# Transposing the softmax weights of 11 heads and three quarters of the feed-forward's tokens with VectorE and HBM in place of TensorE

## The chip, the core and the metric

One core of one Trainium2 chip runs the whole kernel. The metric is device time in microseconds (us). TensorE (PE) multiplies matrices into PSUM and here also transposes 128x128 tiles, VectorE (DVE) and ScalarE (ACT) work elementwise, GpSimd (POOL) helps, and SyncE (SP) issues most of the DMAs. Each engine takes its instructions in order, and the engines wait for each other through semaphores.

## The reference

One layer of an encoder over 256 tokens of width 2048, in float32:

```
h = rmsnorm(x);  q | k | v | u = h @ w_in
scores = q k^T * HEAD_DIM**-0.5 + alibi, masked to |t-s| <= 128
p = exp(scores - m);  p = p / (sum(p) + exp(sink - m))
attention = p v                      (12 query heads, 4 kv heads)
fourier = Re(DFT2(u)) @ w_fourier    (4 groups)
x = x + concat(rmsnorm(attention), rmsnorm(fourier)) @ w_out
g | val = rmsnorm(x) @ w_up;  x = x + (gelu(conv3(g)) * val) @ w_down
y = rmsnorm(x)
```

## The kernel before

Every float32 product is made as three products of rounded halves: an operand is split into `hi` (a copy rounded by ScalarE) and `lo` (the difference, by VectorE). Weights come in units of 1 MB: `load` (line 164) issues the DMA on SP's queue into one of three `raw` buffers, `split` (lines 180 and 181) makes `hi` and `lo`, TensorE multiplies. The order of all work is written out by hand. `unit(i, work)` runs, for unit i: what is listed in `before` (TensorE work of older units), the products of unit i, what is listed in `beside` (VectorE and ScalarE work), `step(i)`, which splits the weights of unit i+2 and then issues the load of unit i+5, and what is listed in `behind`.

Units 0 to 7 are the u and v projections. Units 8 to 23 are the q and k projections, one head each, in the order k, q, q, q for each of four groups. Units 24 to 39 (`N_OUT` is 24) are the output projection, four per chunk of 512 columns. The feed-forward follows.

A query head whose projection is unit s passes through later units: s+1 adds its partial sums (`qk_out`) and splits q (`qk_parts`), s+2 makes the scores on TensorE and, beside them, adds the bias and takes the exponentials (`scores_out`, `exps`), s+3 divides by the sum (`weigh`, line 680), s+4 transposes the 128x512 softmax weights with four TensorE transposes against `ident` (`turn`, line 687) and splits the result out of PSUM into the two tiles `pt` (`turn_out`, lines 699 and 700), s+5 multiplies with v (`values`, line 709) and leaves the result, scaled and split, in a `cat` tile (`values_out`), which the output projection reads. So any unit of the middle stage works on several heads at once.

When a chunk of x is complete (`out_add`, `out_sums`), `turn_x` transposes its 256 tokens by 512 columns with eight TensorE transposes (line 785), and `turn_x_out` scales and splits them into `hT2`, the feed-forward's input (lines 268 and 269). Chunks 0 to 2 do this two units behind the last product; chunk 3 does it in the first step of the feed-forward.

Buffers that matter: `u_hi` and `u_lo` (4 KB per partition each, one buffer) hold the split u until the Fourier group's first product in unit 7; `sc` has four buffers of 2 KB.

Of the kernel before, what the change touches and what calls it, by code (L numbers as in the profile page):

```python
# [8 lines left out]
F32 = mybir.dt.float32  # L9
F32R = mybir.dt.float32r  # L10
AF = mybir.ActivationFunctionType
ALU = mybir.AluOpType

P = 128
D = 2048
S = 256
NK = D // P
HD = 128
NH = 12
# [19 lines left out]
V_G2, V_GA, V_GF, V_DW, V_DB, V_SINK = 0, 16, 28, 32, 161, 204  # L39
# [13 lines left out]
for _g in range(NKV):  # L53
    QK_ORDER += [("k", _g)] + [("q", _g * GQA + _i) for _i in range(GQA)]

QK_FIRST = {n: (2, 2) if n in (8, 12) else (1, 0) for n in range(16)}
N_U, N_V, N_QK = 0, 4, 8
N_OUT = N_QK + len(QK_ORDER)
# [45 lines left out]
def block_kernel(  # L104
# [19 lines left out]
    nc = tc.nc  # L124
    SL = slopes()
    ctx.enter_context(tc.manual_schedule())
    base = ctx.enter_context(tc.tile_pool(name="base", bufs=1))
# [4 lines left out]
    def f32(ap):  # L132
        return ap.bitcast(F32)

    def bank(pool, name):
        return pool.tile([P, 512], F32, tag=pool.name, name=name)
# [29 lines left out]
    def parts_of(i):  # L166
        halves[i] = tuple(
            wp.tile([P, 2176], F32R, tag=h, name=f"{h}{i}", bufs=3)[:, s : s + 2048]
            for h, s in zip(("hi", "lo"), shifts[i])
        )  # L170
        return halves[i]
# [17 lines left out]
    hT = []  # L189
# [10 lines left out]
    xs = [base.tile([P, 2, 512], F32, tag=f"xs{c}", name=f"xs{c}") for c in range(4)]  # L200
# [15 lines left out]
    def u_part(k, o, n, m=1):  # L216

        rows = ux[k // 4][:, (k < 4) * U_HEAD :].rearrange("p (k c) -> p k c", k=4)
        return rows[:, k % 4 : k % 4 + m, o : o + n]
# [43 lines left out]
    def vcol(o, n=1):  # L263
        return vec[:, o : o + n]

    def split_scaled(dst, src, g):

        nc.scalar.activation(dst[:, 0:S], src, AF.Copy, scale=g)
        nc.vector.scalar_tensor_tensor(
            dst[:, S : 2 * S], src, g, f32(dst[:, 0:S]), ALU.mult, ALU.subtract  # L270
        )
# [29 lines left out]
    rows = ctx.enter_context(tc.tile_pool(name="rows", bufs=1, space=bass.MemoryType.DRAM))  # L301

    def row_by_hbm(r, dst, name):
# [2 lines left out]
        nc.gpsimd.dma_start(row.rearrange("b p -> p b"), r)  # L306
        nc.gpsimd.dma_start(dst, row.rearrange("b p -> (b p)").partition_broadcast(P))


    def moving_weights(hi, lo, n, kk, act, b, ps, first, last, q0=0):  # L310

        for q, k in enumerate(kk, q0):
            ah = act(k)[:, b * P : (b + 1) * P]
            al = act(k)[:, S + b * P : S + (b + 1) * P]
            wh, wl = hi[:, q * n : (q + 1) * n], lo[:, q * n : (q + 1) * n]
            nc.tensor.matmul(ps, ah, wh, start=first and q == q0, stop=False)  # L316
            nc.tensor.matmul(ps, al, wh, start=False, stop=False)  # L317
            nc.tensor.matmul(  # L318
                ps, ah, wl, start=False, stop=last and q == q0 + len(kk) - 1
            )  # L320
# [35 lines left out]
    before, beside, behind = {}, {}, {}  # L356

    def at(when, i, f, *a):
        when.setdefault(i, []).append((f, a))
# [13 lines left out]
    for c in range(4):  # L373
        t = base.tile([P, 4, 512], F32R, tag=f"hT{c}", name=f"hT{c}")
        hT.append(t)
    ps_u = [bank(mm, f"ps_u{b}") for b in range(2)]
    for k in range(NK):
        c, q = k // 4, k % 4
        if q == 0:
            hi, lo = (t.rearrange("p (k c) -> p k c", k=4) for t in parts_of(c))  # L380
        n = 1 if c < 2 else 2
# [3 lines left out]
        if q % n == 0:  # L385
            w, h = u_part(k, 0, FW, n), hi[:, q : q + n, :]
# [20 lines left out]
    ph = pa.enter_context(tc.tile_pool(name="pa", bufs=1))  # L407
# [37 lines left out]
    def row_parts(name):  # L445
        return [
            ph.tile([P, 2, FW], F32R, tag=f"{name}_{p}", name=f"{name}_{p}")
            for p in ("hi", "lo")
        ]

    u_hi, u_lo = row_parts("u")
# [157 lines left out]
    qk_sb, st = {}, {}  # L609
    sq_a = ph.tile([P, S], F32, tag="sq", name="sq_a")  # L610

    def qk_out(kind, h, ps):
        tmp = ph.tile([P, S], F32, tag="tmp", name=f"tmp_{kind}{h}", bufs=2)
        nc.scalar.activation(tmp, ps[:, S : 2 * S], AF.Copy)
        add = ph.tile([P, S], F32, tag="add", name=f"add_{kind}{h}", bufs=2)
        nc.vector.tensor_tensor(add, ps[:, 0:S], tmp, ALU.add)
        if kind == "k":
            nc.vector.tensor_tensor(add, add, r1b, ALU.mult)
        st["add", kind, h] = add
# [73 lines left out]
    def turn_out(h):  # L693
# [6 lines left out]
        nc.vector.tensor_tensor(pt[1], ps, f32(pt[0]), ALU.subtract)  # L700
        st["p", h] = pt

    def values(h):
        g = h // GQA
        pt = st.pop(("p", h))
        ps = st["o", h] = bank(dn, f"ps_o{h}")
        for sb in range(2):
            for n, (v, q) in enumerate([(v_hi, 0), (v_hi, 1), (v_lo, 0)]):
                nc.tensor.matmul(  # L709
                    ps[:, 0:S],  # L710
                    v[:, sb, g * HD : (g + 1) * HD],
                    pt[q][:, sb * S : (sb + 1) * S],
                    start=sb == 0 and n == 0,
                    stop=sb == 1 and n == 2,
                )
# [6 lines left out]
    for i in range(N_QK, N_OUT + 8):  # L722
        heads = {i - s: h for (kind, h), s in slot_of.items() if kind == "q"}
        new = [kh for kh, s in slot_of.items() if i - s == 1]
        if 5 in heads:
            at(before, i, values, heads[5])
        if 4 in heads:
            at(before, i, turn, heads[4])
        if 2 in heads:
            at(before, i, scores, heads[2])  # L730
        if 3 in heads:
            at(beside, i, weigh, heads[3])
        for kind, h in new:
            at(beside, i, lambda k=kind, h=h: qk_out(k, h, st.pop(("ps", k, h))))
        if 5 in heads:
            at(beside, i, values_out, heads[5])
        if 4 in heads:
            at(beside, i, turn_out, heads[4])
        for kind, h in new:
            at(beside, i, qk_parts, kind, h)  # L740
        if 2 in heads:
            at(beside, i, scores_out, heads[2])
            at(behind, i, exps, heads[2])

    fourier_channels_steps()
    for n, (kind, h) in enumerate(QK_ORDER):

        def work(hi, lo):
            ps = st["ps", kind, h] = bank(mm, f"ps_{kind}{h}")
            still_weights(hi, lo, ps, range(NK), QK_FIRST[n])  # L750

# [3 lines left out]
    hT2 = []  # L755
# [22 lines left out]
    def turn_x_in(c):  # L778
        pss = []
        for q2 in range(2):  # L780
            ps = bank(dn, f"ps_x{c}{q2}")
            for q in range(2):
                for b in range(2):
                    k4 = 2 * q2 + q
                    nc.tensor.transpose(
                        ps[:, q * S + b * P : q * S + (b + 1) * P],
                        xs[c][:, b, k4 * P : (k4 + 1) * P],
                        ident,
                    )
            pss.append(ps)  # L790
        return pss

    def turn_x_out(c, pss):
        t = base.tile([P, 4, 512], F32R, tag=f"hT{c}", name=f"hU{c}")
        for k4 in range(4):
            ps = pss[k4 // 2][:, k4 % 2 * S : (k4 % 2 + 1) * S]
            split_scaled(t[:, k4, :], ps, vcol(V_G2 + 4 * c + k4))
        hT2.append(t)

    at(before, N_OUT + 6, total, sq_a, "a")  # L800
    at(beside, N_OUT + 6, total_scale, "a", AW)
    ps_a = {}
    for n, (c, kq) in enumerate(OUT_ORDER):
        i = N_OUT + n

        def work(hi, lo):
            if kq == 0:
                ps_a[c] = [bank(mm, f"ps_a{c}{b}") for b in range(2)]
            if kq == 3:
                ps_a[c, "f"] = [bank(dn, f"ps_ff{c}{b}") for b in range(2)]  # L810
            ps = ps_a[c] if kq < 3 else ps_a[c, "f"]
            for b in range(2):
                moving_weights(
                    hi, lo, 512, range(4 * kq, 4 * kq + 4), cat.get, b, ps[b],
                    kq in (0, 3), kq in (2, 3),
                )

        unit(i, work)
        if kq >= 2:
            part = "a" if kq == 2 else "f"  # L820
            ps = ps_a[c] if kq < 3 else ps_a[c, "f"]
            last = c in added
            added.add(c)
            if n == len(OUT_ORDER) - 1:
                later.append(out_post(c, part, ps))
                continue

            at(behind if (c, kq) == (0, 2) else beside, i + 1, out_add, c, part, ps)
            if last:
                at(behind, i + 1, out_sums, c)  # L830
                at(before, i + 2, lambda c=c: st.update({("x", c): turn_x_in(c)}))
                at(beside, i + 2, lambda c=c: turn_x_out(c, st.pop(("x", c))))
    pa.close()
    assert not (before or beside or behind), (before, beside, behind)

# [300 lines left out]
    for q in range(2):  # L1136
        kind, j = items[q]
# [16 lines left out]
    for n, it in enumerate(items):  # L1154
# [8 lines left out]
        if it[0] in ("gate", "val"):  # L1163
            kind, j = it
# [5 lines left out]
        if it[0] == "product":  # L1170
            kind, g, c, p = it
# [13 lines left out]
        else:  # L1185
            kind, c = it
            hi, lo = halves.pop(up_index[n])
# [14 lines left out]
    i = up_index[n]  # L1202
# [35 lines left out]
    x = xs[1][:, 1, :]  # L1238
# [122 lines left out]
```

## Time and profile before

| what | value |
|---|---|
| time, median of 3 runs | 944.87 us (944.45 to 945.13) |
| span of the profiled execution | 943.6 us |
| TensorE busy | 934.2 us, 99% |
| VectorE busy | 759.4 us, 80% |
| ScalarE busy | 542.4 us, 57% |
| GpSimd busy | 50.8 us, 5% |
| granted TensorE clock, mean | 0.998 |
| DMA moved | 214.86 MB |

The profile is one execution. Its span runs from the first to the last instruction; the time of a run includes what lies around that. The page gives busy times by engine and by group of instructions; a group's row names line, engine, operation, output tile<-input tiles, shapes and count, then busy us and mean ns, then the idle time in front of it and what ended it. The chain of waits is the work that ended last, followed back from the last instruction. The timeline lists single instructions with start and length in us; a bracket at its end is the engine's idle time in front of it, with what ended that. DMA rows give the time that SP takes to issue and, apart from it, the time from issue to landing.

### The profile page before, as it was taken

How to read it: one execution, taken by the hardware profiler on the slowest of the kernel's cores; microseconds unless marked ns; L12 is line 12 of the kernel's file. 1: busy time of each engine (PE TensorE's matmuls, PEld its weight loads, DVE VectorE, ACT ScalarE, POOL GpSimd, SP SyncE). 2: the span in 40 equal slices, each digit the busy share in tenths (PEclk: the TensorE clock that was granted, in tenths of full speed). 3: DMA queues.
4: the chain of work that ended last, by engine and by line, in shares of the span. 5: the costliest groups of instructions: out<-in, count | busy, mean ns of one | idle time of the engine just before them, and what ended most of it. 6: DMA issues, size and time to landing. Idle time of an engine off the chain costs nothing.

```text
span 943.6 us, 12812 instructions
## 1 busy us (share of the span) xinstructions
PE 934.2 (99%) x5069; PEld 810.2 (86%) x5069; DVE 759.4 (80%) x946; ACT 542.4 (57%) x662; POOL 50.8 (5%) x68
## 2 busy tenths in 40 slices
PE   9999999999999999999999999999999999999996
PEld 7889998888888888888888888888888888888885
DVE  7658877666677778799887997878989779989886
ACT  7756766554454555566555565555655556655553
POOL 0100000000000000000000000000000000000002
PEclk9999999999999999999999999999999999999999
DMA  9964444445556578877898769877787978779652
GB/s 366 308 223 141 173 140 173 139 174 212 190 215 209 185 232 244 267 257 231 257 266 252 243 236 282 243 262 229 262 242 238 300 245 262 227 234 277 205 179 90
DMA packets 33628, 214.86 MB, mean 228 GB/s; under 512 B 3712, under 2 KB 4224, under 8 KB 10016
## 3 DMA queue, kind: packets, MB, share of 16 engines
q1 hardware_dynamic: 29024, 184.55, 52.8%
q0 software_dynamic: 4544, 29.49, 16.8%
q8 instruction: 40, 0.66, 0.3%
q14 instruction: 20, 0.16, 0.0%
HBM read 211.93 MB, written 2.10 MB: 227 GB/s over the span
## 4 chain that ended last, share of the span: by engine, by line
PE 98%; DVE 1%; DMA 0%; ACT 0%; issue 0%; DVEq 0%; POOLq 0%; POOL 0%; ACTq 0%
PE ps_val L333 25%; PE ps_gate L333 25%; PE ps_q L333 7%; PE ps_P L1070 3%; PE ps_P L1071 3%; PE ps_P L1072 3%; PE ps_N L1070 3%; PE ps_N L1071 3%; PE ps_N L1072 3%; PE ps_a L318 2%; PE ps_k L333 2%; PE ps_a L316 2%; PE ps_a L317 2%; PE ps_s L637 1%; PE ps_o L709 1%; PE ps_ff L316 1%
## 5 line engine op out<-in xcount | busy, mean ns | idle before, releaser
L181 DVE TENSOR_TENSOR lo<-raw,hi 128x2048 fp32r<-128x2048 f32 (+1 forms) x129 | 293.4, 2275 | 44.2 <-ACT hi L180 44.0
L180 ACT ACTIVATE hi<-raw 128x2048 fp32r<-128x2048 f32 (+1 forms) x129 | 245.4, 1903 | 37.8 <-PE ps_a L317 13.5
L333 PE MATMUL ps_val<-hU,hi 128*128 128x512 f32 x688 | 236.2, 389 | 0.0
L333 PE MATMUL ps_gate<-hU,hi 128*128 128x512 f32 x688 | 236.2, 389 | 0.0
L333 PE MATMUL ps_val<-hU,lo 128*128 128x256 f32 x688 | 189.9, 276 | 0.0
L333 PE MATMUL ps_gate<-hU,lo 128*128 128x256 f32 x688 | 189.9, 276 | 0.0
L333 PEld LDWEIGHTS ps_gate<-hU,hi 128*128 128x128 f32 x688 | 129.1, 188 | 26.8
L333 PEld LDWEIGHTS ps_val<-hU,hi 128*128 128x128 f32 x688 | 129.1, 188 | 26.8
L333 PEld LDWEIGHTS ps_gate<-hU,lo 128*128 128x128 f32 x688 | 129.1, 188 | 1.3
L333 PEld LDWEIGHTS ps_val<-hU,lo 128*128 128x128 f32 x688 | 129.1, 188 | 1.3
L845 ACT ACTIVATE ft_g<-ps_gate 128x256 f32<-128x256 f32 x43 | 16.5, 384 | 123.0 <-PE ps_gate L333 123.0
L845 ACT ACTIVATE ft_v<-ps_val 128x256 f32<-128x256 f32 x43 | 16.5, 384 | 91.7 <-PE ps_val L333 91.7
L333 PE MATMUL ps_q<-hT,hi 128*128 128x512 f32 x192 | 65.2, 392 | 0.0
L1070 PE MATMUL ps_P<-hi_P,op_P 128*128 128x512 f32 x144 | 56.0, 389 | 0.0
L1071 PE MATMUL ps_P<-hi_P,op_P 128*128 128x512 f32 x144 | 56.0, 389 | 0.0
L1072 PE MATMUL ps_P<-lo_P,op_P 128*128 128x512 f32 x144 | 56.0, 389 | 0.0
L333 PE MATMUL ps_q<-hT,lo 128*128 128x256 f32 x192 | 51.1, 277 | 0.0
L962 DVE TENSOR_TENSOR lo_N<-sumw,hi_N 128x2048 fp32r<-128x2048 f32 (+1 forms) x20 | 41.5, 2076 | 9.4 <-ACT hi_N L961 9.2
L1070 PE MATMUL ps_N<-hi_N,op_N 128*128 128x512 f32 x108 | 42.0, 389 | 0.0
L1071 PE MATMUL ps_N<-hi_N,op_N 128*128 128x512 f32 x108 | 42.0, 389 | 0.0
L1072 PE MATMUL ps_N<-lo_N,op_N 128*128 128x512 f32 x108 | 42.0, 389 | 0.0
L333 PEld LDWEIGHTS ps_q<-hT,hi 128*128 128x128 f32 x192 | 35.2, 188 | 6.6
(383 smaller groups left out, 1586.9 us busy)
## 6 DMA issues: line engine op xcount, KB each, us to landing
raw<-in_w_up SPq DMA_DIRECT2D x86, 1024.0 KB, 5.8
raw<-in_w_in SPq DMA_DIRECT2D x20, 1024.0 KB, 4.9
raw<-in_w_out SPq DMA_DIRECT2D x16, 1024.0 KB, 4.8
sumw<-in_w_down POOLq DMA_DIRECT2D x16, 1024.0 KB, 8.6
raw<-in_w_down_late SPq DMA_DIRECT2D x4, 1024.0 KB, 6.6
raw<-in_w_down_last SPq DMA_DIRECT2D x4, 768.0 KB, 4.2
ux<-in_w_u_x SPq DMA_DIRECT2D x3, 768.0 KB, 9.2
xs<-in_x SPq DMA_DIRECT2D x4, 512.0 KB, 16.5
```

The lines of the kernel that those rows point to most:

```text
L180: nc.scalar.activation(hi[:, 0:n], raw[:, 0:n], AF.Copy)
L181: nc.vector.tensor_tensor(lo[:, 0:n], raw[:, 0:n], f32(hi[:, 0:n]), ALU.subtract)
L316: nc.tensor.matmul(ps, ah, wh, start=first and q == q0, stop=False)
L317: nc.tensor.matmul(ps, al, wh, start=False, stop=False)
L318: nc.tensor.matmul(ps, ah, wl, start=False, stop=last and q == q0 + len(kk) - 1)
L333: nc.tensor.matmul(ps[:, x], (hi, lo)[i][:, k * P : (k + 1) * P], hk(k)[:, x], start=n == 0 and k == 0, stop=n == len(order) - 1 and k == ...
L637: nc.tensor.matmul(ps[:, b * S : (b + 1) * S], qT[:, qo + b * P : qo + (b + 1) * P], kT[:, ko : ko + S], start=n == 0, stop=n == 2,)
L845: nc.scalar.activation(tmp, ps[:, S : 2 * S], AF.Copy)
L962: nc.vector.tensor_tensor(lo, src, f32(hi), ALU.subtract)
L1070: nc.tensor.matmul(ps, o[:, 0, p, :], hi[:, s], start=first and p == 0, stop=False)
L1071: nc.tensor.matmul(ps, o[:, 1, p, :], hi[:, s], start=False, stop=False)
L1072: nc.tensor.matmul(ps, o[:, 0, p, :], lo[:, s], start=False, stop=last and p == n - 1)
```

## The change

For heads 0 to 10 (`FLIPS`), and for chunks 0 to 2 of x, the TensorE transposes and their PSUM tiles go. In their place VectorE transposes all 32x32 blocks of the tile in one instruction, four DMAs (one per 32 partitions) write these blocks to HBM in runs of 64 floats so that the blocks land in transposed order, and one DMA reads the whole back in runs of 256 floats. The split into `hi` and `lo` then reads SBUF in place of PSUM. Head 11 and chunk 3 stay on TensorE.

For a flipped head, `flip_out` (transpose and writes) stands beside unit s+3, right behind `weigh`; `flip_in` (the read) beside s+4; `flip_parts` (the split) beside s+5; `values` moves from s+5 to s+6. For a chunk, `flip_x_out` stands behind the unit that adds it, `flip_x_in` beside the next and `flip_x_parts` beside the one after. The transposed blocks lie in the buffer of `u_hi` for heads and chunks alike, what comes back in one of `sc` (heads) or in `u_lo` (chunks). All the new DMAs are on SP's queue.

```diff
+FLIPS = range(NH - 1)
...
+    def blocks_out(src, t, name):
+        n = t.shape[1]
+        nc.vector.transpose(t, src)
+        d = rows.tile([n, 32, 4, 64], F32, tag="turn" + name, name="turn" + name, bufs=1)
+        for q in range(4):
+            nc.sync.dma_start(
+                d[:, :, q, :].rearrange("f i r -> i f r"),
+                t[32 * q : 32 * (q + 1)].rearrange("i f b j -> i f (b j)"),
+            )
+        return d
+
+    def blocks_in(d, t):
+        nc.sync.dma_start(t, d.rearrange("(s f) i q r -> (f i) s (q r)", f=4))
...
+    def flip_out(h):
+        sc = st.pop(("sc", h))[0]
+        t = ph.tile([P, 1024], F32, tag="u_hi", name=f"flip{h}")[:, 0:512]
+        t = t.rearrange("p (f b j) -> p f b j", f=8, b=2)
+        st["d", h] = blocks_out(sc.rearrange("p (b f j) -> p f b j", b=2, f=8), t, f"p{h}")
+
+    def flip_in(h):
+        t = ph.tile([P, 512], F32, tag="sc", name=f"flop{h}", bufs=4)
+        t = st["t", h] = t.rearrange("p (s c) -> p s c", s=2)
+        blocks_in(st.pop(("d", h)), t)
+
+    def flip_parts(h):
+        t = st.pop(("t", h)).rearrange("p s (q b j) -> p s b q j", q=4, b=2)
...
+        for s in range(2):
+            nc.scalar.activation(hi[:, s], t[:, s], AF.Copy)
+            nc.vector.tensor_tensor(lo[:, s], t[:, s], f32(hi[:, s]), ALU.subtract)
...
-        if 5 in heads:
-            at(before, i, values, heads[5])
-        if 4 in heads:
+        for n, h in sorted(heads.items()):
+            if n == 5 + (h in FLIPS):
+                at(before, i, values, h)
+        if 4 in heads and heads[4] not in FLIPS:
             at(before, i, turn, heads[4])
...
             at(beside, i, weigh, heads[3])
+            if heads[3] in FLIPS:
+                at(beside, i, flip_out, heads[3])
+        if 4 in heads and heads[4] in FLIPS:
+            at(beside, i, flip_in, heads[4])
...
+        if 5 in heads and heads[5] in FLIPS:
+            at(beside, i, flip_parts, heads[5])
...
+    def flip_x_out(c):
+        t = ph.tile([P, 1024], F32, tag="u_hi", name=f"flipx{c}")
+        t = t.rearrange("p (f b j) -> p f b j", f=16, b=2)
+        src = xs[c].rearrange("p b (f j) -> p f b j", f=16)
+        st["d", "x"] = blocks_out(src, t, f"x{c}")
+
+    def flip_x_in(c):
+        t = ph.tile([P, 1024], F32, tag="u_lo", name=f"flopx{c}")
...
+    def flip_x_parts(c):
...
+        for k in range(4):
...
+            nc.scalar.activation(hi, x[:, k], AF.Copy, scale=g)
+            for b in range(2):
+                nc.vector.scalar_tensor_tensor(
+                    lo[:, b], x[:, k, b], g, f32(hi[:, b]), ALU.mult, ALU.subtract
+                )
...
                 at(behind, i + 1, out_sums, c)
-                at(before, i + 2, lambda c=c: st.update({("x", c): turn_x_in(c)}))
-                at(beside, i + 2, lambda c=c: turn_x_out(c, st.pop(("x", c))))
+                at(behind, i + 1, flip_x_out, c)
+                at(beside, i + 2, flip_x_in, c)
+                at(beside, i + 3, flip_x_parts, c)
```

More of the change, by code (lines that the diff above doesn't have):

```diff
@@ L701, in turn_out @@
         st["p", h] = pt
+    def flip_out(h):
[9 more added lines that the diff above has]
+        t = st.pop(("t", h)).rearrange("p s (q b j) -> p s b q j", q=4, b=2)
+        pt = [
+            ph.tile([P, 512], F32R, tag=f"pt{q}", name=f"pt{q}{h}", bufs=2)
+            for q in range(2)
+        ]
+        hi, lo = (x.rearrange("p (s b q j) -> p s b q j", s=2, b=2, q=4) for x in pt)
+        for s in range(2):
+            nc.scalar.activation(hi[:, s], t[:, s], AF.Copy)
+            nc.vector.tensor_tensor(lo[:, s], t[:, s], f32(hi[:, s]), ALU.subtract)
+        st["p", h] = pt
     def values(h):
@@ L732, in block_kernel @@
             at(beside, i, weigh, heads[3])
+            if heads[3] in FLIPS:
+                at(beside, i, flip_out, heads[3])
+        if 4 in heads and heads[4] in FLIPS:
+            at(beside, i, flip_in, heads[4])
         for kind, h in new:
             at(beside, i, lambda k=kind, h=h: qk_out(k, h, st.pop(("ps", k, h))))
-        if 5 in heads:
-            at(beside, i, values_out, heads[5])
-        if 4 in heads:
+        for n, h in sorted(heads.items()):
+            if n == 5 + (h in FLIPS):
+                at(beside, i, values_out, h)
+        if 4 in heads and heads[4] not in FLIPS:
             at(beside, i, turn_out, heads[4])
+        if 5 in heads and heads[5] in FLIPS:
+            at(beside, i, flip_parts, heads[5])
         for kind, h in new:
@@ L798, in turn_x_out @@
         hT2.append(t)
+    def flip_x_out(c):
[5 more added lines that the diff above has]
+        t = ph.tile([P, 1024], F32, tag="u_lo", name=f"flopx{c}")
+        t = st["x", c] = t.rearrange("p (k c) -> p k c", k=4)
+        blocks_in(st.pop(("d", "x")), t)
+    def flip_x_parts(c):
+        x = st.pop(("x", c)).rearrange("p k (q b j) -> p k b q j", q=4, b=2)
+        t = base.tile([P, 4, 512], F32R, tag=f"hT{c}", name=f"hU{c}")
+        for k in range(4):
+            hi, lo = (
+                t[:, k, p * S : (p + 1) * S].rearrange("p (b q j) -> p b q j", b=2, q=4)
+                for p in range(2)
+            )
+            g = vcol(V_G2 + 4 * c + k)
+            nc.scalar.activation(hi, x[:, k], AF.Copy, scale=g)
+            for b in range(2):
+                nc.vector.scalar_tensor_tensor(
+                    lo[:, b], x[:, k, b], g, f32(hi[:, b]), ALU.mult, ALU.subtract
+                )
+        hT2.append(t)
     at(before, N_OUT + 6, total, sq_a, "a")
```

## The prediction

> **What bounds the kernel now.** I read the page first (span, engines, chain), then the chain of waits by time, then the timelines of VectorE and ScalarE in the projection stage, then the DMA issues.
>
> ```profile
> span 943.6 us, 12812 instructions
> PE 934.2 (99%) x5069; PEld 810.2 (86%) x5069; DVE 759.4 (80%) x946; ACT 542.4 (57%) x662; POOL 50.8 (5%) x68
> PE 98%; DVE 1%; DMA 0%; ACT 0%; issue 0%; DVEq 0%; POOLq 0%; POOL 0%; ACTq 0%
> ```
>
> The chain that ended last is TensorE nearly throughout: what is taken from TensorE is won, if nothing else becomes late. The chain in order of time (start, length, what) gives the price of the transposes:
>
> ```profile
> 78.24 0.72 PE ps_s L637 x6
> ...
> 84.43 0.44 PE ps_t L687 x4
> ...
> 112.35 0.44 PE ps_t L687 x4
> 112.78 0.72 PE ps_s L637 x6
> 113.50 5.45 PE ps_q L333 x32
> 118.95 0.71 PE ps_o L709 x6
> 119.67 0.44 PE ps_t L687 x4
> 120.10 5.48 PE ps_q L333 x32
> ...
> 139.81 0.44 PE ps_t L687 x4
> ...
> 160.38 0.72 PE ps_o L709 x6
> ...
> 187.15 0.71 PE ps_o L709 x6
> ...
> 204.73 0.88 PE ps_x L785 x8
> ```
>
> Each unit is a projection (5.47) with, in front of it, values (`ps_o`, 0.71), transposes (`ps_t`, 0.44 for four) and scores (`ps_s`, 0.72) of older heads. Four units repeat: 112.35 to 139.81 is 27.46 us. VectorE is not idle meanwhile:
>
> ```profile
> core 0: us, PE busy (x) PEld busy (x) DVE busy (x) ACT busy (x) POOL busy (x), PEclk, DMA share, GB/s
> 98.70:126.10 27.40, 27.40 (x178) 24.85 (x176) 22.60 (x51) 18.57 (x36) 2.22 (x3) 1.00 0.44 154
> ```
>
> 22.60 of 27.40 us busy, and much of the rest is waiting inside a ping-pong with ScalarE. That is the second thing to hold against the change. VectorE's timeline, and ScalarE's for the same unit:
>
> ```profile
> 79.81 0.15 DVE L676 TENSOR_TENSOR sm<-sm,ex 128x2 f32<-128x2 f32 x1
> ...
> 86.35 0.16 DVE L676 TENSOR_TENSOR sm<-sm,ex 128x2 f32<-128x2 f32 x1
> ...
> 92.66 0.15 DVE L676 TENSOR_TENSOR sm<-sm,ex 128x2 f32<-128x2 f32 x1
> ...
> 99.64 0.42 DVE L616 TENSOR_TENSOR add_q<-ps_q,tmp_q 128x256 f32<-128x256 f32 x1
> 99.98 0.48 DVE L269 SCALAR_TENSOR_TENSOR cat<-ps_o,vec,cat 128x256 fp32r<-128x256 f32 x1
> ...
> 118.65 0.15 DVE L676 TENSOR_TENSOR sm<-sm,ex 128x2 f32<-128x2 f32 x1
> ...
> 119.04 0.62 DVE L680 TENSOR_SCALAR sc<-sc,ex 128x256 f32<-128x256 f32 x2
> 119.57 0.42 DVE L616 TENSOR_TENSOR add_q<-ps_q,tmp_q 128x256 f32<-128x256 f32 x1
> ...
> 121.70 0.69 DVE L700 TENSOR_TENSOR pt<-ps_t,pt 128x512 fp32r<-128x512 f32 x1 [1.00 <-ACT pt L699]
> 122.31 0.41 DVE L269 SCALAR_TENSOR_TENSOR qT<-add_q,qT 128x256 fp32r<-128x256 f32 x1
> 123.81 2.29 DVE L181 TENSOR_TENSOR lo<-raw,hi 128x2048 fp32r<-128x2048 f32 x1 [1.09 <-ACT hi L180]
> 126.09 0.42 DVE L616 TENSOR_TENSOR add_q<-ps_q,tmp_q 128x256 f32<-128x256 f32 x1
> ```
>
> ```profile
> 120.79 0.39 ACT L472 ACTIVATE sq<-ps_o 128x256 f32<-128x256 f32 x1 [0.61 <-DVE cat L269]
> 121.07 0.59 ACT L699 ACTIVATE pt<-ps_t 128x512 fp32r<-128x512 f32 x1
> 121.55 0.42 ACT L268 ACTIVATE qT<-add_q 128x256 fp32r<-128x256 f32 x1
> 121.86 1.92 ACT L180 ACTIVATE hi<-raw 128x2048 fp32r<-128x2048 f32 x1
> ```
>
> From start to start, where nothing waits: weigh 0.92 (118.65 to 119.57), add 0.34, `cat` 0.48, then ScalarE's `sq`, `pt`, `qT` (0.28, 0.48, 0.31) and `hi` (1.95 until `lo` starts), then `lo`, 2.2 to 2.3. It is a ring: ScalarE can't split the next weights before VectorE has done its add and `cat`, and VectorE can't make `lo` before. This round took 7.4 us (118.65 to 126.09), TensorE's unit 6.6 (0.71 + 0.44 + 5.48).
>
> **What is removed.** 68 of the 80 `transpose` calls of L687 and L785 (44 of 48, 24 of 32): 11 x 0.44 + 3 x 0.88 = 4.84 + 2.64 = 7.5 us of TensorE, all on the chain. With nothing late that is 944.87 - 7.5 = 937.4. The sums are made against the span of 943.6; the median shown is 1.3 above it, and I carry that over.
>
> **What is added, heads.** On VectorE one block transpose (T) of 128x512 behind weigh, and two conversions of 128x256 (each about the 0.42 of `add_q`, 0.34 from start to start) for the one of 0.69; on ScalarE two of about 0.42 (the `qT` row) for 0.59. No row shows T. Nearest rows: `pt`, 128x512, 0.61 from start to start; below, 0.35 if it ran as the 0.31 halves of L680; above, twice `pt` or the row of 1024 columns:
>
> ```profile
> L976 DVE TENSOR_TENSOR sumw<-rawd00a,rawd00b 128x1024 f32<-128x1024 f32 x1 | 1.2, 1219 | 0.0
> ```
>
> I take 0.61 and 0.12 more, since T reads what weigh has just written and can't overlap its end: 0.73 on the ring.
>
> The slots run k, q, q, q, so there are four kinds of unit, by the projection that VectorE takes over in it. Each one's ring after the change, from the lengths above (`kT` as `qT`; half a `pt` on ScalarE as a `qT`):
>
> - the k's: weigh 0.92, T 0.73, two adds 0.79, `cat` 0.48, `sq` 0.28, `kT` 0.33, `hi` 1.95, `lo` 2.2: 7.7
> - the first q's: weigh 0.92, T 0.73, add 0.42, `qT` 0.35, `hi` 1.95, `lo` 2.2: 6.6 (its conversions run beside)
> - the second q's: add 0.34, `cat` 0.51, `sq` 0.28, two halves 0.62, `qT` 0.31, `hi` 1.95, `lo` 2.2: 6.2
> - the third q's: as the second's, with weigh and T: 7.9
>
> Sum 28.4, and each must wait for the one before it. TensorE's units are 6.9, 5.5, 6.9, 6.9 (5.47 with values and scores, the second without either), 27.46 - 3 x 0.44 = 26.1. So here the ring of VectorE and ScalarE becomes the bound.
>
> It doesn't show at once, since VectorE may be late: TensorE wants of a unit only its `pt` and `qT`, for the next unit's values and scores. In the third q's unit the second half of `pt` is there 3.9 us behind weigh's start (the same sum up to the halves, and 0.45 + 0.42 for VectorE's part), in the first q's 2.7. Start of weigh (S) and start of TensorE's unit (P), from S = 79.81, P = 78.24 at unit 12, a third q's, with the first flip (the rings of the next two were 6.54 and 6.31 without T or conversions: 79.81, 86.35, 92.66):
>
> - units 12 to 15: S 79.8, 87.1, 94.1, 100.7; P 78.2, 84.4, 90.6, 96.8 (its values wait 0.4 for `pt`)
> - units 16 to 19: S 106.9, 114.8, 122.5, 129.1; P 103.7, 110.8, 117.7, 125.2 (2.0 late)
> - units 20 to 23: S 135.3, 143.2, 150.9, 157.4; P 132.1, 139.2, 146.1, 153.6 (2.0 late)
> - unit 24: P 160.5, where it stood at 160.38.
>
> Behind it, without new projections, VectorE catches up; the unit that began at 187.15 with 0.71 of values gets 1.42 (heads 10 and 11) and begins at 186.5; both end near 193.4. Net of the heads: +0.1, not -4.84. Every 0.1 us of T moves this by about 1.
>
> **Their DMAs.** Four writes per head (L317 of the diff) and one read on SP's queue, ahead of the weight load of L164 that waits for `lo`, and each T waits for the four writes before it (one buffer, `u_hi`); weigh, add and split of the next unit queue behind that wait.
>
> ```profile
> L230 SPq DMA_DIRECT2D xs<-in_x x4: 541/598/1607, 7.7 to 13.3; - x4
> ...
> DMA to landing us min/median/max: 15.1/16.5/18.0
> ```
>
> ```profile
> L164 SPq DMA_DIRECT2D raw<-in_w_out x16: 327/328/328, 132.8 to 227.0; - x16
> ```
>
> ```profile
> DMA to landing us min/median/max: 1.9/2.3/2.7
> ```
>
> The first view is of `xs`, the load with the most runs in this trace (256; it queued behind megabytes), the second of the weights (128 runs), the last of `out_y`, whose nine writes are each about as large as a head's four together. A DMA of 256 runs takes SP 0.54 to issue, so the four are out 2.2 us behind T, and landed by 4.5. The next T comes 7.1 us behind the end of this one. Up to 7.1 they cost nothing; the bounds are 1.9 and 16.5, and I take 4.5, nearest to `out_y`. The read goes out behind them and is down some 1 us before ScalarE wants it (if not, `qT`, `hi` and the exponentials stand behind it). SP is through by S + 4.5, before its weight load can go. `flop` is a further user of the four `sc` buffers; each is free a unit or more before it is taken again, so that costs nothing, nor do the flipped heads' values, which come one unit later and are first used by the output projection (head 10's stand in unit 28, as head 11's do now).
>
> **The tokens.** Three of four chunks: 2.64 off TensorE. T of 1024 columns 1.22; eight half conversions for four on VectorE. The adds end here:
>
> ```profile
> 202.80 1.40 DVE L762 SCALAR_TENSOR_TENSOR xs<-ps_a,rstda,xs 128x512 f32<-128x512 f32 x2
> ```
>
> I read 204.2 as the time at which chunk 0 is whole. T to 205.4; four issues of 512 runs, between 0.33 and 0.97 each (0.54 for 256), I take 0.75: 208.5; landed 209.9, read down at 212.9, 2.6 us into its unit. Conversions 2, adds 1.4, split 2.3: 218.7. T of chunk 1 to 219.9, down at 227.4, 6.2 into its unit; ScalarE's conversions and `hi`, VectorE's `lo` then end at 233.0, and unit 36 wants it at 232.6: 0.5 lost. At 0.97 an issue it is 3.0, at 0.54 nothing. Chunk 2 has 3 us to spare.
>
> Sum: +0.1 - 2.64 + 0.5 = -2.0; span 941.6, time 942.8.
>
> **Rivals.**
>
> 1. *The ring has more room than I give it*: T at 0.3, as the L680 halves, TensorE stays the bound. By the same sums heads -4.0, tokens -2.6: 938.2, and 937.4 at the very least. For it: 4.8 us of 27.4 were idle; against: the idle time is waiting inside the ring.
> 2. *T is dear* (1.25 on the ring, the 1024 row): heads +5.8, sum 948.6. The Trainium skill, page "VectorE: DVE Perf Modes", section "The three transpose paths", gives 311 ns for 128x128 on VectorE; four of these, an estimate, are 1.24. No row here shows a block transpose.
> 3. *The other side: the write isn't down when the next T wants the buffer.* VectorE then stands before T, with add and both splits behind it. It decides from 7.1 us of landing. Seven T's follow a flip in the unit before; at 8.1 us it is 7 x 1.0: 949.8. For it: one `xs` issue of 1.61; four such make 6.4 + 2.3. Against: 2.3 for as many bytes in `out_y`.
> 4. *The copy in short runs is slow in itself*, not only issued late: a landing as `xs` had, 16.5, is 9.4 past the limit, seven times: over 1000. Against it: `xs` waited in the queue, `out_y` didn't. The Trainium skill, page "VectorE: DVE Perf Modes", section "The three transpose paths", warns that a plain DMA whose access pattern does a transpose by strides is 19 times slower than the transposing one; here the runs stay 256 bytes whole, and no run shows it.
> 5. *The tokens' reads are later* (0.97 per issue): 3.0 for 0.5: 945.3.
>
> **Numbers.** Forecast (ring-bound heads, tokens won) 0.55, its own range 940.5 to 945.5, two thirds of it below 942.98; rival 1 0.10, 2 0.10, 3 0.17, 4 0.02, 5 0.06. About 0.2% (1.9 us) is what a measurement of this kernel can tell from no change. Faster: 0.36 + 0.10 = 0.46; same: 0.19 + 0.06 = 0.25; slower: 0.29. Range 938 to 950, from rival 1 to rival 3: half of rival 3, rival 4 and the lowest part of rival 1 lie outside.
>
> **What would show it.** The chain after: `ps_x` once, `ps_t` once, and between 95 and 170 pieces of VectorE (`lo` of the flipped weights, T) and ScalarE in it, TensorE idle for some 4 to 5 us, mostly in front of `ps_o` two units behind each k. T's mean near 0.7 and 1.2. VectorE nearly full from 80 to 165. T waiting for DMA: under 1 us in all (rival 3 wrong); `pt` waiting for the read: under 1. TensorE waiting near 232 for a `lo`: under 1 (rival 5 wrong). It would be wrong if TensorE has no gaps there (rival 1), or if T waits for DMA each time.

## The result, and the profile after

| | us |
|---|---|
| before, median of 4 runs (lowest to highest) | 944.83 (944.45 to 945.13) |
| changed kernel, median of 4 runs | 952.86 (952.15 to 954.61) |
| ratio, 95% interval | 1.0086 (1.0073 to 1.0098) |
| forecast (range) | 942.8 (938.0 to 950.0) |
| span of the profiled execution, before and after | 943.6, 952.8 |

The change costs 8.0 us where 2 were to be won, and the time lies above the range. The profiled execution is the slowest of the four (954.61); its first group of projections was already 1.1 us late when it ended (at 12.6 us, while the inputs were still coming in), ahead of everything that was changed. So its trace shows what happens; sizes are taken from medians.

The changed kernel's page: span, busy time and the shares of the chain that ended last.

```profile
span 952.8 us, 12850 instructions
...
PE 933.0 (98%) x5001; PEld 805.3 (85%) x5001; DVE 771.5 (81%) x983; ACT 540.5 (57%) x673; POOL 50.8 (5%) x68
...
PE 77%; DVE 9%; DMA 5%; ACT 4%; issue 3%; SPq 1%; DVEq 0%; POOLq 0%; ACTq 0%; POOL 0%
```

TensorE has 68 instructions fewer and is busy 1.2 us less, not 7.5: some of what is left runs slower. The chain, TensorE's for 98% before, now goes through VectorE, ScalarE and DMAs for about a fifth of the span. The waits (engine, line, whom it waited for: us in all, times, longest) say where:

```profile
ACT hU L868 <- DMA flopx<-turnx: 27.8, 3, 10.7
...
PE ps_o L749 <- DVE pt L740: 4.1, 5, 1.5
...
PE ps_a L333 <- ACT hi L181: 3.7, 1, 3.7
...
ACT pt L739 <- DMA flop<-turnp: 3.5, 3, 2.0
...
PE ps_a L335 <- DVE lo L182: 1.3, 1, 1.3
```

The `ps_o` row is the heads, five waits of TensorE. The first row is the tokens: ScalarE stands for 27.8 us in front of three conversions (`hU`), for a read (`flopx`) that is not down. The two `ps_a` rows are what this does to TensorE. The chain through it, in order of time (start, length, what):

```profile
206.19 1.26 DVE flipx L314
...
208.92 3.66 DMA turnx<-flipx
212.66 3.87 DMA flopx<-turnx
216.54 0.52 ACT hU L868
...
222.72 1.25 DVE flipx L314
...
225.50 4.37 DMA turnx<-flipx
230.02 4.00 DMA flopx<-turnx
...
234.46 1.29 ACT hU L868 x3
235.75 1.81 ACT hi L181
237.58 2.30 DVE lo L182
239.93 0.79 PE ps_a L335
240.72 0.43 PE ps_a L333
...
244.93 0.23 PE ps_a L334
...
277.45 2.62 PE ps_gate L350 x15
```

Read it upwards: TensorE wants `lo`, `lo` wants `hi`, and `hi` stands in ScalarE's queue behind the conversions of chunk 1, whose data come down only at 234.0. Nobody wants those conversions before the feed-forward. The second thing to see is the 0.43 of a matmul behind the gap, where it takes 0.23 otherwise. The windows of that stretch (columns as in the prediction; the granted clock is the third number from the end):

```profile
core 0: us, PE busy (x) PEld busy (x) DVE busy (x) ACT busy (x) POOL busy (x), PEclk, DMA share, GB/s
...
230.00:235.00 5.00, 3.92 (x18) 2.91 (x16) 0.42 (x2) 0.96 (x3) 0.00 (x0) 1.00 0.68 257
235.00:240.00 5.00, 1.07 (x3) 0.37 (x3) 4.20 (x9) 5.00 (x5) 0.00 (x0) 0.79 0.14 57
240.00:245.00 5.00, 5.00 (x13) 3.91 (x14) 5.00 (x6) 2.03 (x4) 0.00 (x0) 0.53 0.72 231
245.00:250.00 5.00, 5.00 (x24) 4.14 (x23) 3.88 (x3) 2.48 (x3) 0.00 (x0) 1.00 0.86 316
```

TensorE's timeline gives the price. The last matmul ahead of the gap, and the first at the full pace again, are these:

```profile
233.53 0.39 PE L335 MATMUL ps_ff<-lo,cat 128*128 128x512 f32 x1
...
244.76 0.39 PE L334 MATMUL ps_a<-hi,cat 128*128 128x512 f32 x1
```

That is 14 steps from start to start in 11.2 us; at the 0.227 that a step takes ahead of the gap (12 of them from 230.81 to 233.53) they are 3.2. So 8.0 us are lost: 5.0 of them idle time (3.7 and 1.3), about 3 the low clock, which after the gap was granted at half for about 6.8 us ((0.21 + 0.47) x 5 / 0.5). The page "TensorE: Matmul & The Clock Gate" of the Trainium skill, Part 1 on the clock gate, says that an idle window of about 3.4 us halves the clock; the trace agrees in kind (a gap of 3.7, and 0.5). The feed-forward's first unbroken unit of `ps_gate` begins at 277.45, where it stood at 268.72; 1.1 of these 8.7 us are the late start.

The heads, by VectorE's timeline (start, length, what):

```profile
107.94 0.15 DVE L693 TENSOR_TENSOR sm<-sm,ex 128x2 f32<-128x2 f32 x1
...
108.98 0.71 DVE L314 STREAM_TRANSPOSE flip<-sc 128x512 f32<-128x512 f32 x1
109.62 0.39 DVE L633 TENSOR_TENSOR add_q<-ps_q,tmp_q 128x256 f32<-128x256 f32 x1
...
115.90 0.15 DVE L693 TENSOR_TENSOR sm<-sm,ex 128x2 f32<-128x2 f32 x1
...
123.64 0.15 DVE L693 TENSOR_TENSOR sm<-sm,ex 128x2 f32<-128x2 f32 x1
...
130.20 0.42 DVE L633 TENSOR_TENSOR add_q<-ps_q,tmp_q 128x256 f32<-128x256 f32 x1
...
136.52 0.15 DVE L693 TENSOR_TENSOR sm<-sm,ex 128x2 f32<-128x2 f32 x1
```

From round to round 7.96, 7.74, 6.56 and 6.32: the forecast's four rings (7.9, 7.7, 6.6, 6.2), and 28.6 for its sum of 28.4. T is 0.71 long on 512 columns, and 1.24 on 1024:

```profile
L314 DVE STREAM_TRANSPOSE flip<-sc x11: 711/711/712, 81.9 to 174.2; 128x512 f32<-128x512 f32 x11
L314 DVE STREAM_TRANSPOSE flipx<-xs x3: 1239/1242/1245, 206.2 to 246.8; 128x1024 f32<-128x1024 f32 x3
```

### The profile page after: what moved, and what is told of

Same layout as the page of the kernel before. It is cut to its first block, busy times and chain, and to the rows that moved or that the text cites. A ratio compares the mean times of both kernels' runs of the same rounds, so it can differ in the third digit from the quotient of the medians.

```text
span 952.8 us, 12850 instructions
## 1 busy us (share of the span) xinstructions
PE 933.0 (98%) x5001; PEld 805.3 (85%) x5001; DVE 771.5 (81%) x983; ACT 540.5 (57%) x673; POOL 50.8 (5%) x68
## 4 chain that ended last, share of the span: by engine, by line
PE 77%; DVE 9%; DMA 5%; ACT 4%; issue 3%; SPq 1%; DVEq 0%; POOLq 0%; ACTq 0%; POOL 0%
PE ps_val L350 25%; PE ps_gate L350 24%; DVE lo L182 4%; PE ps_P L1146 3%; PE ps_P L1147 3%; PE ps_P L1148 3%; ACT hi L181 3%; PE ps_N L1146 2%; PE ps_N L1147 2%; PE ps_N L1148 2%; DMA turnx<-flipx 1%; DMA flopx<-turnx 1%; PE ps_a L335 1%; PE ps_a L333 1%; PE ps_a L334 1%
## 5 line engine op out<-in xcount | busy, mean ns | idle before, releaser
L333 PE MATMUL ps_a<-hi,cat 128*128 128x512 f32 x96 | 38.6, 402 | 3.7 <-ACT hi L181 3.7
```

## The experiments

Theory A, from the chain above: the loss lies in the tokens, where conversions stand in ScalarE's queue ahead of their data; the heads cost little, since their ring gives back what TensorE saves. Rival B: the heads make VectorE late, and that breaks the tokens. Rival C: the many short transfers themselves slow the rest. Every kernel was timed in turn with the kernel before, whose median was 944.96, 944.91 and 945.14 in the three groups.

### The parts alone

Heads alone:

```diff
-                at(behind, i + 1, flip_x_out, c)
-                at(beside, i + 2, flip_x_in, c)
-                at(beside, i + 3, flip_x_parts, c)
+                at(before, i + 2, lambda c=c: st.update({("x", c): turn_x_in(c)}))
+                at(beside, i + 2, lambda c=c: turn_x_out(c, st.pop(("x", c))))
```

> Heads alone: the weights of 11 heads by VectorE and HBM, all chunks of the tokens on TensorE as before. Theory A (the loss is in the tokens; the heads are bound by the ring of VectorE and ScalarE and TensorE gives back in waits what it saves): 945.7 us, between 945 and 947. Rival B (the heads make VectorE late, and this lateness is what breaks the tokens' stage too): also 945 to 947 here, but then the tokens alone come out as forecast, near 942.5. Rival C (the many short runs slow the weight loads): 948 or more, with TensorE waiting for halves of weights whose load landed late.

Measured: 945.81, ratio 1.0010 (1.0000 to 1.0019).

Tokens alone:

```diff
-FLIPS = range(NH - 1)
+FLIPS = ()
```

> Tokens alone: three chunks by VectorE and HBM, all heads on TensorE as before. Theory A (ScalarE stands in its queue at the conversions of a chunk whose read is not down, with the next weights' halves behind it): 951 us, between 949 and 952.5; TensorE idle for about 5 us in front of the second chunk's successor and at a granted clock near 0.5 for some 5 us after it. Rival B (only lateness out of the heads breaks it): 942 to 943.

Measured: 952.79, ratio 1.0081 (1.0069 to 1.0094); TensorE's gaps 4.2 and 1.1 behind chunk 1 and 1.1 more behind chunk 2, and a granted clock of 0.50 from 235 to 240. So the tokens alone cost 7.8 us (a little above what A expected), the heads 0.85. B falls: with no head turned the tokens are as dear.

### The same transfers, with the conversions one unit later

```diff
-                at(beside, i + 3, flip_x_parts, c)
+                at(beside, i + 4, flip_x_parts, c)
...
-        t = ph.tile([P, 1024], F32, tag="u_hi", name=f"flipx{c}")
+        t = ph.tile([P, 1024], F32, tag="uvu"[c] + "_hi", name=f"flipx{c}")
...
-        t = ph.tile([P, 1024], F32, tag="u_lo", name=f"flopx{c}")
+        t = ph.tile([P, 1024], F32, tag="uvu"[c] + "_lo", name=f"flopx{c}")
```

> The whole change, with the conversions of each chunk one unit later (and, so that this is free, a second pair of buffers). Theory A: no idle TensorE and no low clock in the tokens' stage; the 952.9 lose the 8.3 us that the windows of 230 to 270 show idle or at low clock: 944.6, between 943 and 945.5. Rival C (the transfers themselves take too much): stays above 949.

Measured: 943.12, ratio 0.9983 (0.9974 to 0.9992): at the low end of A's range, and 9.7 us under the change.

The same with no head turned:

> Tokens alone with the conversions one unit later. Theory A: the 2.64 us of TensorE are won whole: 942.2, between 941.5 and 943. Rival B: the same as the tokens alone without the move, whatever that is. Rival C: 947 or more.

Measured: 942.44, ratio 0.9972 (0.9961 to 0.9983). 2.5 us are won of the 2.64 that the transposes took, and TensorE waits for nothing in this stage. ScalarE still stands up to 5.3 us in front of a conversion, which now costs nothing, since the halves that TensorE wants next are made ahead of it. C falls too: the same short transfers are all there.

### The tokens without the way by HBM

The conversions stay where the change has them, but read T's tile; blocks are left out of place.

```diff
-        st["d", "x"] = blocks_out(src, t, f"x{c}")
+        nc.vector.transpose(t, src)
+        st["x", c] = t
...
-        blocks_in(st.pop(("d", "x")), t)
```

> Tokens alone without the way by HBM: the three block transposes and all conversions stay where the change puts them, but the conversions read the transposed tile directly; the blocks are not put in their places and the output is another. If the time from the transpose to the read's landing, in front of ScalarE's queue, is the whole loss: 942.4, as with the conversions one unit later. If the block transposes and half conversions themselves are too much for VectorE there: 946 or more.

Measured: 942.03, ratio 0.9969 (0.9958 to 0.9981). VectorE's added work costs nothing here; the wait for the trip is the whole loss.

### What makes the trip long

In the tokens alone T's writes follow a load of 1 MB of weights that was issued about 1 us earlier. Here T goes ahead of that split and load, in chunks 1 and 2:

```diff
-                at(behind, i + 1, flip_x_out, c)
+                at(beside if c else behind, i + 1, flip_x_out, c)
```

> Tokens alone as in the change, but for chunks 1 and 2 the block transpose and its writes go ahead of the next weights' split and load (2.2 us earlier on VectorE, and the writes ahead of a load of 1 MB on the queue). If the writes land late because a load was issued just before them: their landing behind the last issue falls from 5 to about 2.5 us, the read is down some 5 us earlier, and the time is 945.5, between 944 and 947.5. If short runs land late by themselves: only the 2.2 us are won, about 950.

Measured: 948.13, ratio 1.0033 (1.0020 to 1.0047): between the two. The chain for chunk 1 (T, then the last write from its issue to its landing, then the read), first of the tokens alone, then of this kernel:

```profile
219.37 1.25 DVE flipx L314
...
222.19 5.63 DMA turnx<-flipx
227.96 3.92 DMA flopx<-turnx
```

```profile
217.32 1.26 DVE flipx L314
...
220.03 3.08 DMA turnx<-flipx
223.25 6.37 DMA flopx<-turnx
```

The writes land 2.5 us sooner, as expected, but the load now goes out between writes and read, and the read takes 2.5 longer. The loss moved from one leg of the trip to the other; only the earlier T was won. The time fell by 4.7 all the same, more than the 2.0 by which TensorE's two gaps shrank (from 5.3 to 3.3): with gaps of 1.7 and 1.6 the clock stayed at 1.00 in the profiled execution, so there the half clock's 2.5 us went too. (Its mean clock is 0.998; the other four runs have 0.995 to 0.997.) Next, the read goes out right behind the writes, ahead of any load:

```diff
-                at(beside, i + 2, flip_x_in, c)
+                at(beside if c else behind, i + 1, flip_x_in, c)
```

> Tokens alone, the transpose of chunks 1 and 2 ahead of the split as in the run before it, and the chunk's read issued right behind its writes, so that no load of weights stands between them on the queue. If the read's 5.9 to 6.4 us there came from the load issued just ahead of it: the read lands in 3.8 to 4, about 2.5 us earlier for each of two chunks, TensorE's gaps of 3.3 and about 1 us shrink to 1 and 0, and the time is 945, between 944 and 946. If the transfer takes that long whatever stands ahead: 948 again.

Measured: 944.00, ratio 0.9990 (0.9981 to 0.9999); one gap of 1.4. Its chain:

```profile
217.34 1.26 DVE flipx L314
...
220.06 2.96 DMA turnx<-flipx
223.15 4.33 DMA flopx<-turnx
```

So a load of 1 MB ahead of a leg costs that leg about 2 to 2.7 us (the read 6.37 for 4.33 and 3.92, the writes 5.63 for 3.08 and 2.96). From T's end to the read's landing it is 8.9 us with no load ahead, still 1.4 above the forecast's 7.5; why is not shown.

### The heads: the ring or the reads?

T made twice in each of the 11 heads:

```diff
         nc.vector.transpose(t, src)
+        nc.vector.transpose(t, src)
```

> Heads alone with VectorE's block transpose made twice. If the ring of VectorE and ScalarE bounds the heads, each of the 11 second transposes (0.64 to 0.71) lands on it whole: 945.8 + 7.0 to 7.8 = 953, between 952 and 954. If the heads wait for the transfers instead, VectorE has room for it: under 948.

Measured: 953.78, ratio 1.0096 (1.0081 to 1.0110), 7.97 above the heads alone: 0.72 for each T. In VectorE's timeline the rounds that hold a T are longer by 0.74 to 0.77, the fourth round by nothing. TensorE's longer waits brought its clock to half in this trace (below), but the time does not hang on that: one of the five runs kept a mean clock of 0.997 and took 954.40. Then the heads without the way by HBM (the conversions read T's tile, taken from the `sc` buffers):

```diff
-        st["d", h] = blocks_out(sc.rearrange("p (b f j) -> p f b j", b=2, f=8), t, f"p{h}")
+        nc.vector.transpose(t, sc.rearrange("p (b f j) -> p f b j", b=2, f=8))
+        st["t", h] = u.rearrange("p (s c) -> p s c", s=2)
...
-        blocks_in(st.pop(("d", h)), t)
```

> Heads alone without the way by HBM: the transpose stays, the conversions read its tile directly, so that the blocks are not put in their places and the output is another. If the ring bounds the heads, the transfers are hidden and it stays at 945.8, between 944.5 and 946. If TensorE's waits come from reads that are down too late: under 942.5 (the 4.84 us of TensorE won, less a little).

Measured: 945.91, ratio 1.0011 (1.0002 to 1.0020), and TensorE's wait is the same to the tenth as in the changed kernel (there against L740, here L739):

```profile
PE ps_o L748 <- DVE pt L739: 4.1, 5, 1.5
```

So the 55 transfers of the heads are hidden and the ring is the bound.

### A version that beats both

If the ring binds only where it is longer than TensorE's unit, a head whose T falls into a short ring can be turned for nothing. With the tokens' conversions one unit later:

```diff
-FLIPS = range(NH - 1)
+FLIPS = (2, 5, 8)
```

> The tokens with conversions one unit later, and only the heads 2, 5 and 8 by VectorE, whose block transpose falls into the shortest of the three rings that hold one. If the ring bounds only where TensorE's unit is shorter than it: 3 x 0.44 are won on 942.44: 941.1, between 940.6 and 941.8. If each head so turned costs its share of what the eleven cost (0.85 over 11): 942.7.

Measured: 940.97, ratio 0.9958 (0.9945 to 0.9970), 4.2 us under the kernel before. From its page:

```profile
span 939.2 us, 12831 instructions
...
PE 929.9 (99%) x5033; PEld 805.9 (86%) x5033; DVE 764.8 (81%) x967; ACT 541.5 (58%) x665; POOL 50.8 (5%) x68
...
PE 98%; DVE 1%; DMA 0%; ACT 0%; issue 0%; DVEq 0%; POOLq 0%; POOL 0%; ACTq 0%
```

The chain is TensorE's again. Other sets of heads were not tried: this run does not tell whether these three are free because their T falls into a short ring, or because only one head in four is turned.

## Why the prediction was wrong, step by step

- **Removed work.** 2.64 of the tokens and 3 x 0.44 of three heads came back as 2.5 and 1.5 us where nothing became late. Right.
- **T.** 0.71 for 128x512, 1.24 for 1024 columns, 0.72 on the ring (7.97 over 11): the forecast took 0.73 and 1.22. Rivals 1 (0.3) and 2 (1.25) are out. The 311 ns of the Trainium skill beside rival 2 (page "VectorE: DVE Perf Modes", section "The three transpose paths") stand there for bf16; T here is float32, and the measured 0.71 decides.
- **The ring and its table.** Four rings of 28.6 for 28.4; TensorE waits 4.1 us in all for 4 to 5. The two waits of 1.5 stand in front of units 19 and 23, where the table has its 2.0; three of 0.4 stand in front of units 17, 21 and 25, which it does not have, and its 0.4 in front of unit 15 did not come. Right in the main.
- **"Behind it, without new projections, VectorE catches up".** Wrong by 0.75: heads +0.85 for +0.1. In the heads alone the chain begins:

```profile
53.90 5.48 PE ps_k L350 x32
...
167.66 0.86 PE ps_o L749 x5
...
186.84 1.43 PE ps_o L749 x12
```

  The kernel before has its first k here:

```profile
54.33 1.83 PE ps_k L333 x10
```

  The heads alone started 0.43 earlier, so against 187.15 the last unit stands at 186.84 + 0.43 = 187.27, for a forecast of 186.5. Most of the missing 0.77 is in unit 25, whose values waited once more for their softmax weights, VectorE's half of `pt` (first matmul at 166.92, the rest from 167.66): VectorE was not through with unit 24. Up to there the table held: unit 24 began at 160.02 + 0.43 = 160.45, for 160.5.
- **The heads' transfers.** Writes landed 2.3 to 5.4 us after their issue and no T waited for them: rivals 3 and 4 are out. The read was not always down a microsecond early; ScalarE waited for it three times, 3.5 in all. That this costs nothing is shown by the run without HBM.
- **The tokens: the failed step.** "Landed 209.9, read down at 212.9", "down at 227.4", "0.5 lost", "Chunk 2 has 3 us to spare". The order of events was right, and chunk 1 was the one named, but the trip from T's end to the read's landing was sized at 7.5 us and took 9.1, 10.1 and 10.4 (writes down after 5.1 to 6.2, for 4.5; reads 3.9 to 4.1 behind their issue, for 3.0). The issues, the only term that was given bounds, took 2.2 to 2.8 for four, under the 3.0 taken. It is the landings that were too short, and they had no bounds, though a load of weights goes out ahead of them. The last write was to land 2.2 behind the start of its issue (207.7 to 209.9), as `out_y`, which stands at the kernel's end; it took 3.7, 4.4 and 4.5. For the read's 3.0 the prediction shows no row. A nearer one was in its view of the weights' loads, which land so (most of them 1 MB):

```profile
DMA to landing us min/median/max: 4.1/5.1/18.1
```

  In the tokens alone T of chunk 1 began at 219.4, close to the forecast's 218.7; its read was down at 231.9 for 227.4, a trip of 11.3. Nearly every microsecond beyond a point already 0.5 late was lost one for one: with the read down 2.3 and 4.4 earlier, in the two kernels with T ahead of the split, the two gaps of 5.3 together shrank by 2.0 and 3.9. Chunk 2 had nothing to spare either: in the tokens alone TensorE waited 1.1 behind it.
- **What was not in the sum at all.** The half clock behind the gap, some 2.5 to 3 us. Rival 5 had the right wait, a read that comes too late for unit 36, but laid it to slow issues, which were faster than taken; without the slow landings and without the clock it came to 945.3.
- **The cause, shown from both sides.** Without the trip, or with the trip as it is and the conversions one unit later, the same tokens win 2.9 and 2.5 us: it is the trip's length against the place of its reader in the queue, and nothing else in the tokens' part.

## What to carry to other kernels

An instruction that waits for a transfer belongs in an engine's queue behind the work that the bounding engine wants next, unless the transfer is surely down by then: here one unit's delay was worth 10 us, though ScalarE still waited up to 5.3 for a read. A transfer's time is to be taken from rows with the same traffic ahead of it, with an upper bound, and a gap of a few microseconds on TensorE priced with the slower clock behind it. Before moving work off a bounding engine, compare its unit with the ring that takes the work: three heads were turned for nothing, eleven cost more than they saved.

## What the runs showed that was not expected

The half clock came from a shorter gap than the 3.4 us that the Trainium skill gives (page "TensorE: Matmul & The Clock Gate", Part 1). With T made twice, TensorE's longest wait is 2.8 us:

```profile
PE ps_o L750 <- DVE pt L741: 7.7, 3, 2.8
```

and the window behind the second of the three shows the clock:

```profile
130.00:132.00 2.00, 2.00 (x11) 2.00 (x11) 0.71 (x2) 2.00 (x3) 0.00 (x0) 0.52 1.01 259
```

The shortest of the three waits, 2.2, brought it to 0.84 over the window of 98 to 100. Two gaps of 1.7 and 1.6, in the profiled execution with T ahead of the split, left it at 1.00. Whether such a gap brings the half clock each time is open: of the five runs with T made twice four have a mean clock of 0.993, and one, as slow as they are, has 0.997, as the kernel before; only one of the five was traced.
